# Adding up the seven products of a Winograd-form FFN-down matmul: three running sums kept as they are, one kept combined, and every addition on VectorE

## The chip, the cores and the metric

The kernel runs on one NeuronCore of a Trainium2 chip. The metric is the device time of one execution in microseconds (us); a lower time is better. A core has five engines that run side by side and wait for each other through semaphores: TensorE (PE; its weight loads are shown apart as PEld), VectorE (DVE), ScalarE (ACT), GpSimd (POOL) and SyncE (SP), which issues the DMAs here. Matmul results land in PSUM, from where VectorE and ScalarE read them; everything else lies in SBUF or in HBM.

## The reference

One layer of a diffusion backbone over 640 tokens (512 latent, 128 context): a mixer (gated DeltaNet and latent attention), then a gated convolutional FFN, then a final norm. The part that matters here is the end:

```python
def conv_ffn(h, w_up, conv_w, conv_b, w_down):
    u = depthwise_conv_centred(h @ w_up, conv_w) + conv_b
    a, gate = jnp.split(u, 2, axis=-1)
    return (jax.nn.silu(a) * gate) @ w_down
...
    x = x + gate2 * conv_ffn(h2, p['w_up'], p['ffn_conv_w'], p['ffn_conv_b'], p['w_down'])
```

D_MODEL is 2048 and D_FF is 5632, all in float32. `@ w_down` is the "down" stage: for each of 16 output tiles (128 features x 640 tokens) it sums over 44 tiles of 128 hidden features.

## The kernel before

**The seven products.** Down works on 2x2 blocks. A pair of output tiles p (8 pairs) and the two halves of the tokens (320 each) make four output quarters C11, C12, C21, C22 of 128x320; four hidden tiles at a time (index n, 11 of them) make the inner dimension. Instead of eight block products it computes seven, Q1 to Q7, from sums of weight blocks and sums of activation blocks (Winograd's form), and then combines them: C11 = Q1+Q2, C12 = Q1-Q6-Q5+Q3, C21 = -Q4-(Q1-Q6+Q7), C22 = Q5-(Q1-Q6+Q7), each summed over n. Float32 precision is kept by splitting every operand into a high and a low part (`split`, L921: a cast on ScalarE writes `whi` or `b_hi`, a subtraction on VectorE writes `wlo` or `b_lo`), and each product is three matmuls: hi by hi, hi by lo, and lo by hi.

**Units.** For one (p, n) the work is two units: R computes Q2, Q1, Q4, Q7 with the raw weight blocks (24 matmuls of 128x320 into two PSUM tiles named `mm`), S computes Q6, Q5, Q3 with the weight sums (18 matmuls into two PSUM tiles named `dn`). The table `blocks` (L1479) sets the order: a plain first block (4 units W, without Winograd), then blocks 1 to 8 with two n for each of four p, block 9 with three n and block 10 with two. Within a block PSUM accumulates over its n; so for every p, 40 times in all, the seven products have to be added to the running sums in SBUF before the next p may write the same PSUM. This text calls the work on one p of one block a round.

**The running sums** are tiles `x_hi`, `x_lo` and `xw` (the first two are named for the freed activation buffers that they occupy); c11, c12, c21, c22 are halves of two of them.

**Around it**, for each unit: `d_load` (L1528) brings 512 KB of weights into `wraw` (2 buffers); `d_sums` (L1533) makes three weight sums and one difference with four 128x256 additions on VectorE (tiles `us` and `vs`); `d_prep` (L1542) splits the weights (2 buffers of `whi`, `wlo`); `g_prep` (L1511), spread over a block by `g_steps`, makes four differences of activations per tile on GpSimd (L1518; tiles `ca`, `cg`, `rawa`, `rawg`, `graw`) and splits them; `residual2` (L1655) adds the gated result to x behind the last block of a p, with one GpSimd addition (L1670).

**The adding up** is `d_post` (L1607), called for the unit before the one whose matmuls were just issued. All its additions are recorded by the helper `add`, so they stand at line L1603, as do those of `d_sums`. Behind R, ScalarE copies Q1 and Q7 to tiles `x` and `y` (L1624, L1625) and VectorE adds Q2 and Q1 to c11 and subtracts Q4 from c21, three reads of PSUM. Behind S, VectorE makes x = x - Q6 and y = y + x, subtracts Q5 from c12, adds Q3 to c12 and Q5 to c22; GpSimd adds x to c12 and subtracts y from c21 and from c22. In block 1, where c11 to c22 of four p start, the first write replaces the sum (`new`).

**What sets the order.** A scheduler puts each engine's instructions into a fixed list when the program is built; each engine then goes through its list in order and waits where a semaphore is not yet there. PSUM tiles `mm` are single (two tags, one buffer each), so the first R of a round waits until VectorE and ScalarE have read the last R of the round before.

## Time and profile before

| | |
|---|---|
| median of 3 runs | 3340.32 us (3339.84 to 3347.75) |
| profiled execution, its own time | 3335.4 us |
| its span, first to last instruction | 3333.6 us |
| busy over the span: PE, DVE, ACT, POOL | 93%, 82%, 44%, 19% |
| mean granted TensorE clock | 0.965 of full speed |
| down stage in the trace | about 2684 to 3307 us |

A busy share says how long an engine's instructions ran, with the waiting inside an instruction counted as running. The down stage is the last fifth; the rows below are nearly all from it. "Idle before" is the time in which an engine stood still ahead of an instruction, put down to what released it.

### The profile page before, as it was taken

The numbers are of one execution on the slowest core, as the hardware profiler recorded it, in microseconds if no ns is written. First come the engines' busy times: TensorE is split into PE (matmuls) and PEld (weight loads), VectorE is DVE, ScalarE is ACT, GpSimd is POOL, SyncE is SP. The second block draws the span as 40 slices with busy tenths as digits, with TensorE's granted clock in tenths as the row PEclk, the third lists the DMA queues.
The fourth block names the chain that finished last, engine by engine and source line by source line (L and its number), as shares of the span: only waits on it lengthen the run. The fifth ranks groups of instructions, "written<-read, shape, count | busy, mean of one in ns | idle before, by whom it ended". The sixth has DMA issues, their size and how long they took to land. (4 is left out here: it accounts for less than half of the span.)

```text
span 3333.6 us, 54622 instructions
## 1 busy us (share of the span) xinstructions
PE 3099.1 (93%) x21243; PEld 2989.7 (90%) x21243; DVE 2721.6 (82%) x4626; ACT 1450.2 (44%) x2230; POOL 640.5 (19%) x456
## 2 busy tenths in 40 slices
PE   5889999999998998997999999999999989889996
PEld 4688989898998988997999999999999988888986
DVE  7766666866576667998998898898898889999988
ACT  5444555554446542115544444444444443333433
POOL 1211111211110001334100010000000044334323
PEclk9999999998899999998999999999999999999998
DMA  7652222323233217873333333333333333232333
GB/s 274 212 173 75 81 83 69 104 66 98 70 120 98 63 64 238 283 257 108 129 123 105 114 125 105 121 125 99 126 118 98 108 116 100 86 103 91 95 107 119
DMA packets 181475, 403.93 MB, mean 121 GB/s; under 512 B 39392, under 2 KB 57952, under 8 KB 181216
## 3 DMA queue, kind: packets, MB, share of 16 engines
q1 hardware_dynamic: 181216, 400.44, 37.3%
q8 instruction: 167, 2.74, 0.3%
q14 instruction: 92, 0.75, 0.1%
HBM read 361.83 MB, written 38.54 MB: 120 GB/s over the span
## 5 line engine op out<-in xcount | busy, mean ns | idle before, releaser
L922 ACT CAST whi<-wraw 128x1024 fp32r<-128x1024 f32 x256 | 268.9, 1050 | 521.6 <-PE mm L1596 200.4
L326 DVE SCALAR_TENSOR_TENSOR aacc<-araw,csil,aacc 128x512 f32<-128x512 f32 x510 | 397.3, 819 | 14.2 <-DMA araw<-in_w_ada_dram 13.7
L198 PE MATMUL mm<-b_hi,whi 128*128 128x320 f32 x1344 | 398.6, 310 | 4.7 <-ACT whi L922 3.9
L198 PE MATMUL mm<-b_lo,whi 128*128 128x320 f32 x1344 | 397.7, 310 | 0.0
L923 DVE TENSOR_TENSOR wlo<-wraw,whi 128x1024 fp32r<-128x1024 f32 x256 | 326.0, 1273 | 81.4 <-PE dn L207 63.0
L131 POOL TENSOR_TENSOR wlo<-wraw,whi 128x1024 fp32r<-128x1024 f32 x61 | 191.3, 3135 | 982.4 <-PE mm L207 553.0
L198 PE MATMUL mm<-h_hi,whi 128*128 128x320 f32 (+1 forms) x1312 | 326.7, 328 | 7.7 <-ACT h_hi L289 6.2
L198 PE MATMUL mm<-h_lo,whi 128*128 128x320 f32 (+1 forms) x1312 | 316.3, 321 | 12.5 <-POOL h_lo L290 12.5
L198 PE MATMUL dn<-b_lo,whi 128*128 128x320 f32 x1008 | 297.7, 309 | 0.0
L198 PE MATMUL dn<-b_hi,whi 128*128 128x320 f32 x1008 | 297.6, 309 | 0.0
L1596 PE MATMUL mm<-b_hi,whi 128*128 128x320 f32 x672 | 216.9, 335 | 60.2 <-DVE x_hi L1603 27.8
L129 ACT CAST whi<-wraw 128x1024 fp32r<-128x1024 f32 (+1 forms) x138 | 142.8, 1034 | 268.8 <-PE mm L198 164.8
L198 PEld LDWEIGHTS mm<-b_hi,whi 128*128 128x128 f32 x1344 | 253.2, 188 | 5.5 <-ACT whi L922 4.4
L198 PEld LDWEIGHTS mm<-b_lo,whi 128*128 128x128 f32 x1344 | 253.2, 188 | 0.0
L198 PEld LDWEIGHTS mm<-h_lo,whi 128*128 128x128 f32 x1312 | 227.5, 194 | 16.3 <-POOL h_lo L290 14.8
L198 PEld LDWEIGHTS mm<-h_hi,whi 128*128 128x128 f32 x1312 | 226.9, 195 | 13.3 <-ACT h_hi L289 8.2
L207 PE MATMUL mm<-h_hi,wlo 128*128 128x320 f32 (+1 forms) x1312 | 236.8, 322 | 0.0
L1456 POOL TENSOR_TENSOR y<-x,y 128x320 f32<-128x320 f32 x42 | 40.7, 968 | 977.1 <-DVE x L1454 977.1
L207 PE MATMUL mm<-b_hi,wlo 128*128 128x320 f32 x1344 | 224.4, 309 | 0.0
L922 ACT CAST whi<-us 128x1024 fp32r<-128x1024 f32 (+1 forms) x126 | 123.5, 980 | 230.8 <-PE mm L198 162.7
L1596 PE MATMUL mm<-b_lo,whi 128*128 128x320 f32 x672 | 210.0, 329 | 0.0
L207 PEld LDWEIGHTS mm<-h_hi,wlo 128*128 128x128 f32 x1312 | 206.4, 195 | 1.8
(534 smaller groups left out, 7895.0 us busy)
## 6 DMA issues: line engine op xcount, KB each, us to landing
wraw<-in_w_up_dram SPq DMA_DIRECT2D x176, 512.0 KB
araw<-in_w_ada_dram SPq DMA_DIRECT2D x272, 256.0 KB
wraw<-in_w_down_dram SPq DMA_DIRECT2D x88, 512.0 KB
wraw<-in_w_in_dram SPq DMA_DIRECT2D x80, 512.0 KB
araw<-in_w_ada_dram SPq DMA_DIRECT2D x56, 512.0 KB
wraw<-in_w_out_dram SPq DMA_DIRECT2D x32, 512.0 KB
graw<-g_d SPq DMA_DIRECT2D x44, 320.0 KB
g_d<-cg SPq DMA_DIRECT2D x44, 256.0 KB
```

Source lines behind the costliest of these rows:

```text
L129: act.copy(hi[:, :, 0:n], raw[:, :, 0:n])
L131: (pool if on_pool else dve).tensor_tensor(lo[:, :, 0:n], raw[:, :, 0:n], hi.bitcast(F32)[:, :, 0:n], ALU.subtract)
L198: pe.matmul(o, wts[0][:, k, col:col + P], m[:, sl], start=start and k + n == 0, stop=False)
L207: pe.matmul(o, wts[1][:, k, col:col + P], mov(k)[0][:, sl], start=False, stop=stop and k == 3)
L326: dve.scalar_tensor_tensor(acc[:, c, 0:w], raw, vecs[:, kt, c:c + 1], acc[:, c, 0:w], ALU.mult, ALU.add)
L922: act.copy(dst_hi, src)
L923: dve.tensor_tensor(dst_lo, src, dst_hi.bitcast(F32), ALU.subtract)
L1456: pool.tensor_tensor(y, x, y, ALU.add)
L1596: pe.matmul(dq[q], wt(w[0], k), bs[(2 * n + k) % 6][m][:, q, :], start=n == grp[0] and k + m == 0, stop=False)
```

## The change

Three things change in the down stage, and one tile is laid out differently in the up stage.

1. The running sums are C11, C12+C22, C21 and C22. Since C12+C22 = Q3 - Q7, no product is read twice: Q1 comes to c11 from ScalarE's copy, and Q5 goes to c22 alone. After the plain block c22 is added to c12 (4 additions), and after a p's last block it is subtracted again (8 additions).
2. `d_post` now only reads PSUM; a new `d_post2` does the additions between SBUF tiles, all on VectorE. x, y and z are three slices of one tile `xyz`, and ScalarE copies Q7 with its sign changed. So c11 and c12, where they lie side by side in one tile, take x and -Q7 in one addition of 128x640; c21 and c22 take the third slice in one 128x640 subtraction. For pair p = 6 they don't lie side by side, and there it is four of 128x320. In block 1 ScalarE copies Q2, Q4, Q3 and Q5 into the sums.
3. `d_sums` is called between `d_post` and `d_post2` and no longer in `d_prep`.

```diff
--- before.py
+++ after.py
@@ -1441,16 +1441,14 @@
         q24, q17, q53, q6 = (pq.get((p, n)) for n in (0, 1, 2, 6))
         half = (slice(0, CH), slice(512, 512 + CH))
         if g == 4:
-            x = cp.tile([P, CH], F32, name="x")
-            y = cp.tile([P, CH], F32, name="y")
-            tt[p] = (x, y)
+            xyz = cp.tile([P, 3, CH], F32, name="xyz")
+            tt[p] = x, y, _ = [xyz[:, n] for n in range(3)]
             act.copy(x, q17[:, half[0]])
             act.copy(y, q17[:, half[1]])
             dve.tensor_tensor(raws[0][:, 1:CH + 1], x, q24[:, half[0]], ALU.add)
             dve.tensor_tensor(raws[1][:, 1:CH + 1], y, q24[:, half[1]], ALU.subtract)
         if g == 6:
-            x, y = tt.pop(p)
-            z = cp.tile([P, CH], F32, name="z")
+            x, y, z = tt.pop(p)
             dve.tensor_tensor(x, x, q6[:, half[0]], ALU.add)
             dve.tensor_tensor(z, x, q53[:, half[0]], ALU.add)
             pool.tensor_tensor(y, x, y, ALU.add)
@@ -1552,7 +1550,6 @@
             split(hi, lo, draw[i])
             d_load(i + 2)
         if c != "R":
-            d_sums(i + 1)
             draw.pop(i)
         return hi, lo
 
@@ -1604,51 +1601,70 @@
 
     dt = {}
 
-    def d_post(u, q):
-
+
+
+    def d_done(u):
         i, c = units[u]
         b, p, n = order[i]
         if n != blocks[b][1][-1]:
+            return None
+        return c, b, p, n, [xh[2 * p + m // 2][m % 2] for m in range(4)]
+
+    def d_post(u, q):
+
+        if not d_done(u):
             return
+        c, b, p, n, (c11, c12, c21, c22) = d_done(u)
         if c == "W":
             for t, ps in zip((2 * p, 2 * p + 1), q):
                 for x, sl in x_pieces(t):
                     act.copy(x, ps[:, C0 + sl.start:C0 + sl.stop])
-            return
-        new = b == 1
-        c11, c12, c21, c22 = (xh[2 * p + m // 2][m % 2] for m in range(4))
-        if c == "R":
-            x = cp.tile([P, CH], F32, name="x")
-            y = cp.tile([P, CH], F32, name="y")
-            dt[p] = (x, y)
-            act.copy(x, q[Q1])
-            act.copy(y, q[Q7])
-            if new:
-                add(dve, c11, x, q[Q2])
-                dve.scalar_tensor_tensor(c21, y, -1.0, q[Q4], ALU.mult, ALU.subtract)
+        elif c == "R":
+            dt[p] = xyz = cp.tile([P, 3, CH], F32, name="xyz")
+            act.copy(xyz[:, 0], q[Q1])
+            act.activation(xyz[:, 1], q[Q7], AF.Copy, scale=-1.0)
+            if b == 1:
+                act.copy(c11, q[Q2])
+                act.activation(c21, q[Q4], AF.Copy, scale=-1.0)
             else:
                 add(dve, c11, c11, q[Q2])
-                add(dve, c11, c11, q[Q1])
                 add(dve, c21, c21, q[Q4], ALU.subtract)
+        else:
+            xyz = dt[p]
+            add(dve, xyz[:, 2], xyz[:, 0], q[Q6], ALU.subtract)
+            if b == 1:
+                act.copy(c12, q[Q3])
+                act.copy(c22, q[Q5])
+            else:
+                add(dve, c12, c12, q[Q3])
+                add(dve, c22, c22, q[Q5])
+
+    def d_post2(u):
+
+        if not d_done(u):
             return
-        x, y = dt.pop(p)
-        add(dve, x, x, q[Q6], ALU.subtract)
-        if new:
-            add(dve, c12, x, q[Q5], ALU.subtract)
-            add(pool, y, x, y)
-            add(dve, c12, c12, q[Q3])
-            add(pool, c21, c21, x, ALU.subtract)
-            add(dve, c22, q[Q5], y, ALU.subtract)
-        else:
-            add(dve, y, y, x)
-            add(dve, c12, c12, q[Q5], ALU.subtract)
-            add(dve, c12, c12, q[Q3])
-            add(dve, c22, c22, q[Q5])
-            add(pool, c12, c12, x)
-            add(pool, c21, c21, y, ALU.subtract)
-            add(pool, c22, c22, y, ALU.subtract)
-        if n == 10:
-            finish.append(p)
+        c, b, p, n, (c11, c12, c21, c22) = d_done(u)
+        if c == "W":
+            add(dve, c12, c12, c22)
+        elif c == "S":
+            xyz = dt.pop(p)
+            add(dve, xyz[:, 2], xyz[:, 2], xyz[:, 1], ALU.subtract)
+            y = xyz[:, 2]
+            if 2 * p in xw:
+                w = xw[2 * p].rearrange("p (h c) -> p h c", h=2)
+                add(dve, w, w, xyz[:, 0:2])
+            else:
+                add(dve, c11, c11, xyz[:, 0])
+                add(dve, c12, c12, xyz[:, 1])
+            if 2 * p + 1 in xw:
+                w = xw[2 * p + 1].rearrange("p (h c) -> p h c", h=2)
+                add(dve, w, w, y.unsqueeze(1).broadcast_to([P, 2, CH]), ALU.subtract)
+            else:
+                add(dve, c21, c21, y, ALU.subtract)
+                add(dve, c22, c22, y, ALU.subtract)
+            if n == 10:
+                add(dve, c12, c12, c22, ALU.subtract)
+                finish.append(p)
 
     finish, sq, xres = [], {}, {}
 
@@ -1792,6 +1808,10 @@
         w = w2
         if u:
             d_post(u - 1, q0)
+        if u + 1 < len(units) and units[u + 1][1] != "R":
+            d_sums(units[u + 1][0] + 1)
+        if u:
+            d_post2(u - 1)
         q0 = q
         if finish and units[u][1] == "S":
             done = finish.pop(0)
@@ -1805,6 +1825,7 @@
             r_load(0)
             r_load(1)
     d_post(len(units) - 1, q0)
+    d_post2(len(units) - 1)
     for i in range(2):
         sq[14 + i] = raws[i][:, 0:T]
     sums = ps_pair(0)
```

**In the instruction lists.** Counted over the down stage, VectorE had 312 additions of 128x320 for the adding up, 276 of them with a PSUM operand; it now has 256 of 128x320, 184 of them with a PSUM operand, and 70 of 128x640. GpSimd had 116 and has none. The up stage's lists are the same but for the tile's name.

VectorE, block 2, from the end of one round to the start of the next; `mm` and `dn` are PSUM. Before:

```order
L1603 TENSOR_TENSOR vs<-wraw,vs 128x256
L1603 TENSOR_TENSOR x_lo_26652<-x_lo_26652,mm_27709 128x320
L923 TENSOR_TENSOR wlo<-wraw,whi 128x1024
L1603 TENSOR_TENSOR x_lo_26652<-x_lo_26652,mm_27710 128x320
L1603 TENSOR_TENSOR x_lo_26652<-x_lo_26652,mm_27709 128x320
L1603 TENSOR_TENSOR x<-x,dn 128x320
L923 TENSOR_TENSOR wlo<-us,whi 128x768
L1603 TENSOR_TENSOR y<-y,x 128x320
L1603 TENSOR_TENSOR x_lo_26652<-x_lo_26652,dn 128x320 x3
L1603 TENSOR_TENSOR us<-wraw 128x256
L1603 TENSOR_TENSOR us<-us,wraw 128x256
```

Now:

```order
L1600 TENSOR_TENSOR x_lo_26570<-x_lo_26570,mm_27618 128x320
L923 TENSOR_TENSOR wlo<-wraw,whi 128x1024
L1600 TENSOR_TENSOR x_lo_26570<-x_lo_26570,mm_27618 128x320
L1600 TENSOR_TENSOR vs<-wraw,vs 128x256
L1600 TENSOR_TENSOR xyz<-xyz,dn 128x320
L923 TENSOR_TENSOR wlo<-us,whi 128x768
L1600 TENSOR_TENSOR x_lo_26570<-x_lo_26570,dn 128x320 x2
L1600 TENSOR_TENSOR xyz<-xyz 128x320
L1600 TENSOR_TENSOR x_lo_26570<-x_lo_26570,xyz 128x640 x2
L923 TENSOR_TENSOR wlo<-wraw,whi 128x1024
L1600 TENSOR_TENSOR us<-wraw 128x256
L1600 TENSOR_TENSOR us<-us,wraw 128x256
```

Between the split of the next R (`wlo<-wraw`) and the last read of `mm` stood two reads, and now one; behind the split of the next S (`wlo<-us`) stood y and three reads of `dn`, and now two reads, one addition of 128x320 and two of 128x640.

GpSimd, in blocks 6 and 7: `ca` and `cg` belong to the two activation tiles of one step. Before:

```order
L1518 TENSOR_TENSOR ca<-graw,ca 128x320
L1518 TENSOR_TENSOR rawa<-ca,graw 128x320
L1603 TENSOR_TENSOR xw_26654<-xw_26654,y 128x320
L1603 TENSOR_TENSOR xw_26653<-xw_26653,x 128x320
L1603 TENSOR_TENSOR xw_26654<-xw_26654,y 128x320
L1603 TENSOR_TENSOR x_hi_26649<-x_hi_26649,y 128x320
L1603 TENSOR_TENSOR x_hi_26649<-x_hi_26649,x 128x320
L1603 TENSOR_TENSOR x_hi_26649<-x_hi_26649,y 128x320
L1518 TENSOR_TENSOR cg<-graw 128x320
L1518 TENSOR_TENSOR graw<-graw 128x320
L1518 TENSOR_TENSOR cg<-graw,cg 128x320
```

Now:

```order
L1516 TENSOR_TENSOR ca<-graw,ca 128x320
L1516 TENSOR_TENSOR rawa<-ca,graw 128x320
L1516 TENSOR_TENSOR cg<-graw 128x320
L1516 TENSOR_TENSOR graw<-graw 128x320
L1516 TENSOR_TENSOR cg<-graw,cg 128x320
```

The six additions between the two groups of four are gone, and the groups follow each other.

ScalarE, block 1, the end of the first round. Before:

```order
L922 CAST whi<-wraw 128x1024
L1624 COPY x<-mm_27015 128x320
L1625 COPY y<-mm_27015 128x320
L922 CAST whi<-us 128x768
L922 CAST whi<-wraw 128x1024
L922 CAST whi<-vs 128x768
```

Now:

```order
L922 CAST whi<-wraw 128x1024
L1627 COPY x_hi_26567<-mm_26928 128x320
L1624 COPY xyz<-mm_26929 128x320
L1625 ACTIVATE xyz<-mm_26929 128x320
L1628 ACTIVATE x_hi_26567<-mm_26928 128x320
L922 CAST whi<-us 128x768
L1636 COPY x_hi_26567<-dn 128x320
L1637 COPY x_hi_26567<-dn 128x320
L922 CAST whi<-wraw 128x1024
```

ScalarE now reads all of the first block's PSUM tiles but Q6.

## Rows read from the trace of the kernel before

**Rows 1.** windows: whole down stage, a free round, one block (columns as headed).
```profile
core 0: us, PE busy (x) PEld busy (x) DVE busy (x) ACT busy (x) POOL busy (x), PEclk, DMA share, GB/s
2684.00:3307.00 623.00, 558.69 (x3557) 544.72 (x3556) 565.23 (x915) 236.59 (x342) 235.06 (x198) 0.96 0.30 96
2850.70:2863.00 12.30, 12.30 (x86) 12.30 (x85) 11.93 (x21) 8.83 (x15) 3.73 (x3) 1.00 0.35 112
2850.70:2909.10 58.40, 52.47 (x338) 50.88 (x337) 55.40 (x89) 22.12 (x33) 21.74 (x20) 0.97 0.29 95
```

**Rows 2.** waits, 2690 to 3310: engine line waited for: total us, times, longest.
```profile
PE mm L1596 <- DVE x_hi L1603: 27.8, 18, 3.0
...
PE mm L1596 <- DVE x_lo L1603: 15.6, 7, 3.0
...
PE mm L1596 <- ACT xw L1616: 8.0, 1, 8.0
...
PE mm L1596 <- DVE x_hi L1628: 3.5, 2, 2.6
```

**Rows 3.** lines by form, DVE, down stage: xcount | busy us, mean ns | idle before.
```profile
L923 DVE TENSOR_TENSOR wlo<-wraw,whi 128x1024 fp32r<-128x1024 f32 x84 | 115.8, 1379 | 18.4 <-PE mm L1599 13.4 <-ACT whi L922 2.1 <-ACT cg L1668 1.8
L923 DVE TENSOR_TENSOR wlo<-vs,whi 128x768 fp32r<-128x768 f32 x42 | 44.5, 1059 | 7.2 <-PE dn L1599 7.2
...
L923 DVE TENSOR_TENSOR b_lo<-graw,b_hi 128x640 fp32r<-128x640 f32 x38 | 36.9, 974 | 0.0
L1603 DVE TENSOR_TENSOR us<-wraw 128x256 f32<-128x256 f32 x41 | 31.3, 764 | 4.6 <-DMA wraw<-in_w_down_dram 4.6
...
L1603 DVE TENSOR_TENSOR x_hi<-x_hi,mm 128x320 f32<-128x320 f32 x57 | 26.1, 476 | 0.0
...
L1603 DVE TENSOR_TENSOR vs<-wraw,vs 128x256 f32<-128x256 f32 x42 | 18.1, 431 | 0.0
L1603 DVE TENSOR_TENSOR y<-y,x 128x320 f32<-128x320 f32 x35 | 16.8, 480 | 0.0
...
L923 DVE TENSOR_TENSOR b_lo<-ca,b_hi 128x640 fp32r<-128x640 f32 x9 | 7.3, 810 | 0.0
```

**Rows 4.** line L1603 alone, down stage: duration ns shortest/median/longest.
```profile
L1603 DVE TENSOR_TENSOR x_hi<-x_hi,mm x57: 472/475/489, 2765.9 to 3292.4; 128x320 f32<-128x320 f32 x57
...
L1603 DVE TENSOR_TENSOR us<-wraw x41: 408/743/1102, 2700.0 to 3279.7; 128x256 f32<-128x256 f32 x41
...
L1603 POOL TENSOR_TENSOR x_lo<-x_lo,y x41: 866/887/1866, 2771.1 to 3297.3; 128x320 f32<-128x320 f32 x41
```

**Rows 5.** the weight splits alone, down stage, the same columns.
```profile
L923 DVE TENSOR_TENSOR wlo<-wraw,whi x84: 1207/1224/1939, 2690.5 to 3298.5; 128x1024 fp32r<-128x1024 f32 x84
```

**Rows 6.** timeline, 2898.9 to 2902.7: start us, us, engine line op names.
```profile
2898.91 1.40 DVE L1603 TENSOR_TENSOR x_lo<-x_lo,dn 128x320 f32<-128x320 f32 x3
...
2899.06 0.87 POOL L1603 TENSOR_TENSOR x_lo<-x_lo,y 128x320 f32<-128x320 f32 x1 [5.48 <-DVE y L1603]
...
2899.99 0.87 POOL L1603 TENSOR_TENSOR x_lo<-x_lo,x 128x320 f32<-128x320 f32 x1
2900.22 0.91 DVE L1603 TENSOR_TENSOR us<-wraw 128x256 f32<-128x256 f32 x1
```

**Rows 7.** windows of line L1603 alone, down stage.
```profile
core 0: us, DVE busy (x) POOL busy (x), PEclk, DMA share, GB/s
2684.00:3307.00 623.00, 312.00 (x636) 125.07 (x113) 0.96 0.30 96
```

**Rows 8.** windows of line L1518 alone (GpSimd differences of activations), down stage.
```profile
2684.00:3307.00 623.00, 0.00 (x0) 81.43 (x72) 0.96 0.30 96
```

**Rows 9.** lines by form, ACT, down stage.
```profile
L1625 ACT COPY y<-mm 128x320 f32<-128x320 f32 x40 | 17.3, 431 | 0.0
```

**Rows 10.** the chain that ended last, its piece behind the last product.
```profile
3306.60 0.50 DVE x L1603
...
3307.69 0.87 POOL xw L1603
```

## The prediction

> **What bounds the kernel now.** The up stage's instruction lists stay as they are, so I read the down stage only, first by windows. Over its 623 us TensorE is busy for 558.7, VectorE for 565.2 and GpSimd for 235.1 [rows 1]: two engines are nearly full, and neither sets the pace alone. A free round shows TensorE's pace: 12.30 us, busy throughout at the full clock [rows 1], for 84 matmuls, so 0.146 us each. One steady block of four rounds takes 58.4 us, 9.2 more than four times 12.30 = 49.2. [...] VectorE is idle for only 3.0 of the 58.4.
>
> The waits, read next, tell what TensorE stands idle for: VectorE's additions to the running sums, 27.8 + 15.6 us in 25 times, then 8.0 behind ScalarE's copies of the plain block and 3.5 in block 1 behind L1628 [rows 2]. All are the first matmul on `mm`: a round cannot start before the last round's R products are read. In VectorE's list that last read stands behind a weight split and two other reads.
>
> Third, why VectorE is late. Groups by form, against the shortest of their kind, show that some of its instructions run far longer than they need: the first weight sum takes 764 ns in the mean [rows 3] and 408 at best [rows 4], while a read of PSUM takes 476 [rows 3], with 472 and 489 as ends [rows 4]. The timeline shows what lies beside the long ones: three reads of PSUM run through while GpSimd works, 1.40 us for three, but a sum of two SBUF tiles of 256 columns takes 0.91 us behind GpSimd's addition [rows 6].
>
> **The change, part by part.** All durations are of the profiled execution, 3335.4 us with a span of 3333.6; the median shown is 3340.3, so what comes out below is subtracted from the median too.
>
> *VectorE's own work: +30 us.* Before, 312 additions by 0.476 [rows 3] are 148.5 us. Now 256 by 0.476 are 121.9, and 70 of 640 columns by 0.810 (the subtraction `b_lo<-ca` has that width [rows 3]) are 56.7; together 178.6. An addition without PSUM costs the same as one with it (`y<-y,x` 480 [rows 3]), so trading one for the other is free by itself.
>
> [...]
>
> *GpSimd's additions beside VectorE: -43 us.* Mean less shortest, by count: the seven groups of weight sums (first and last in rows 3, shortest about 408 [rows 4]) come to 61 us, the R weight splits to 84 x (1379 - 1207) = 14 [rows 3, 5], the activation splits to 38 x (974 - 810) = 6 [rows 3]; 81 us in all that VectorE's instructions are held up beside GpSimd. GpSimd is busy 125.1 us with the adding up [rows 7] out of 235.1 [rows 1]: 53%, so 43 us. Ends: 19, if each of the 72 activation differences [rows 8] already holds VectorE for its whole 0.866 [rows 4], 62 us; and 81, if they hold nothing.
>
> *More VectorE work that GpSimd can hold up: +7 us.* What is left of GpSimd's work (81.4 us of differences [rows 8] and 13 residual additions) now costs 81 - 43 = 38. Before, 276 x 0.476 = 131 of VectorE's 565 us were reads of PSUM, which are not held up; now it is 184 x 0.476 = 88. So 77% of its time was exposed and 84% will be: +4. The wide additions are the longest exposed ones, so I take +7. Ends: -3, when the groups of four, no longer queued behind additions that wait for y, fall into VectorE's idle tenth; and +34, when each of the 72 holds it for a whole 0.866 (62 instead of their share of 38, which is 28).
>
> VectorE's load thus changes by 30 - 43 + 7 = -6 us, with ends at -51 (30 - 81) and +21 (30 - 43 + 34). One round in four is bound by TensorE, as the free one is; three quarters count: **-4.5**.
>
> *One read fewer before the release: -8.* Between the split of the next R and the last read of `mm` stood two reads, now one; a read in a row takes about 0.45 (1.40 for three [rows 6]). TensorE waited there 25 times [rows 2]: 11 us at most. In a round that VectorE fills from end to end the place in the list does not matter, so I take two thirds. Behind the next S split the list gets longer (four instructions of 0.45 before, three and two of about 0.75 now: +1.0), in a place where `mm` is already free; it is covered as long as TensorE's R and S units, 42 x 0.146 = 6.1 us, run beside it.
>
> *Block 1: -3.* Its reads of `mm` go to ScalarE, four of 0.431 [rows 9] are 1.7 us, covered by the S unit's 18 x 0.146 = 2.6. The 3.5 us behind L1628 [rows 2] should nearly go.
>
> *Plain block: +1.* Four more VectorE additions are 1.9 us if its list there is full; TensorE's 8.0 wait hangs on ScalarE and stays. Between 0 and 1.9. *Tail: +1.* From VectorE's x at 3306.60 to the end of GpSimd's addition at 3308.56 [rows 10] it is 2.0 us; now four additions of 0.45 and two of 0.75 stand there, 3.3. Nothing covers it.
>
> *Clock: -4.* The whole stage needs 3720 matmuls (84 times 42, and 192 of the plain block) x 0.146 = 545 us and TensorE is busy 558.7: 14 us at the lower level beside 55 of waits, 0.25 per us of wait. On -4.5 - 8 - 3 that is -4.
>
> Sum: -4.5 - 8 - 3 + 1 + 1 - 4 = -17.5, say -17. Profiled 3318, median **3323 us**. ScalarE's extra copies (16 of 128x320, and a sign at no cost) are hidden: it is busy 237 of 623 [rows 1].
>
> **The rivals.**
>
> *Larger gain, 3303.* If the additions taken from GpSimd had cost VectorE 60 rather than 43 and nothing comes back, the load falls by 30, x 0.75 = -22; the full 11 for the read, -3, +2 and a quarter of 36 for the clock make -43. VectorE would then more often be ahead of its weights (it waits 4.6 us for their DMA before one of the sums even now [rows 3]), so I call it -37. For it: the long sums lie right behind GpSimd's additions [rows 6]. Against: three fifths of the stage's GpSimd instructions cannot well cost three quarters of the delay.
>
> *No change, 3338.* The wait moves: the weight sums now stand behind the reads and, for `us`, behind the wide additions too, and ScalarE's cast of the next R waits for their last difference. TensorE then waits for `whi` instead of `mm`, the 8 and the clock's share are lost, and -2 remains. For it: VectorE is as full as before. Against: a cast of weights is not among TensorE's largest waits today [rows 2].
>
> *Slower, 3365.* The remaining differences, in uninterrupted groups of four, hold up the wide additions. If all 72 cost their 0.866, VectorE's load rises by 21 and it is behind in every round, so all of it counts, with a quarter for the clock: +26, no gain from the order, -3 + 2: +25. It decides from 13 us of growth instead of my 7, where the load stops falling. For it: VectorE has 3.0 of 58.4 us to spare. Against: today's differences cost 28 of 62.
>
> [...]
>
> **How the numbers follow.** Within 0.3%, 10 us, this kernel's measurement cannot be told from no change. Forecast 0.46 (own range 3313 to 3333: faster 0.38, same 0.08); no change 0.27 (same 0.22, faster 0.03, slower 0.02); larger 0.15 (faster); slower 0.12 (slower 0.10, same 0.02). Together 0.56, 0.32 and 0.12. The range 3299 to 3348 takes in the forecast, no change and most of the larger gain, and leaves out the slower rival's far end.
>
> **What would show it.** Right: the weight sums' means near 550 ns or less, VectorE busy about 560 us in the stage, TensorE's waits for L1603's successors under 30 us, no wait at block 1, wide additions at 0.81 to 0.95 in the mean. Wrong: wide additions above 1.1 us in the mean (slower), or TensorE waiting for `whi` (no change). The up stage must end at 2684 as before; if it does not, the difference isn't in this argument.

## The result, and the profile after

The changed kernel takes 3301.5 us (median of 4 runs, 3283.3 to 3303.2), the kernel before 3342.1 in the same series: ratio 0.9864, 95% interval 0.9827 to 0.9901, so it is 33 to 58 us faster; the medians differ by 41. The forecast was 17 faster: the direction was right, its size less than half of the measured one.

First the place. This row shows the first matmuls of the plain block (ns shortest, median and longest, then the starts of the first and the last in us), of the kernel before:

```profile
L1572 PE MATMUL mm<-b_hi,whi x32: 304/309/413, 2659.4 to 2683.0; 128*128 128x320 f32 x32
```

and of the changed kernel:

```profile
L1569 PE MATMUL mm<-b_hi,whi x32: 309/309/414, 2674.2 to 2697.7; 128*128 128x320 f32 x32
```

The down stage starts 14.8 us later after the change, though nothing ahead of it was to change. The change is not needed to explain that: in the fourteen other traces below, whose instructions are nearly the same up to there, the stage starts anywhere from 2662 to 2677, and 14 of the 14.8 us arise in the first 300 us of the program. The plain block itself takes 28.5 us in both. So I compare the forty rounds, from the last matmul of the plain block to the last product, by windows; the kernel before:

```profile
core 0: us, PE busy (x) PEld busy (x) DVE busy (x) ACT busy (x) POOL busy (x), PEclk, DMA share, GB/s
2688.00:3307.10 619.10, 554.79 (x3530) 541.05 (x3530) 561.32 (x912) 236.13 (x341) 231.22 (x195) 0.96 0.30 96
```

and the changed kernel, one steady block and all rounds:

```profile
2861.60:2912.20 50.60, 49.91 (x339) 49.44 (x339) 50.06 (x90) 22.21 (x33) 10.81 (x8) 1.00 0.36 110
2702.70:3269.70 567.00, 532.02 (x3528) 525.76 (x3528) 536.70 (x921) 240.01 (x354) 112.75 (x82) 0.98 0.34 105
```

The rounds take 567.0 instead of 619.1: -52.1. What follows them, the tail, takes 30.7 instead of 26.5. Together that is -48 in one trace of each kernel, against -41 of the medians with an interval 25 wide, so the rounds hold the whole effect as far as these can tell. A block that took 58.4 [rows 1] takes 50.6, with TensorE (49.9) and VectorE (50.1) both nearly full.

TensorE's waits in the rounds of the changed kernel (total us, times, longest), which answer to [rows 2]:

```profile
PE mm L1593 <- DVE x_lo L1600: 9.5, 9, 5.2
PE mm L1593 <- ACT xw L1621: 8.8, 1, 8.8
PE mm L1593 <- DVE x_hi L1600: 7.0, 5, 2.5
PE mm L1593 <- ACT whi L922: 4.0, 3, 1.4
PE mm L1593 <- DVE xyz L1600: 3.6, 2, 1.9
```

Behind x_hi and x_lo it is 16.5 instead of 43.4, block 1 has none, and the plain block's wait behind ScalarE stays (8.8). VectorE's groups by form (count | busy, mean ns | idle before), which answer to [rows 3]:

```profile
L923 DVE TENSOR_TENSOR wlo<-wraw,whi 128x1024 fp32r<-128x1024 f32 x84 | 107.8, 1283 | 9.8 <-ACT whi L922 6.0 <-PE mm L1596 3.5
...
L1600 DVE TENSOR_TENSOR x_hi<-x_hi,xyz 128x640 f32<-128x640 f32 x30 | 25.0, 861 | 0.0
...
L1600 DVE TENSOR_TENSOR x_lo<-x_lo,xyz 128x640 f32<-128x640 f32 x30 | 23.6, 814 | 0.0
L1600 DVE TENSOR_TENSOR vs<-wraw 128x256 f32<-128x256 f32 x42 | 22.3, 532 | 13.4 <-DMA wraw<-in_w_down_dram 13.4
...
L1600 DVE TENSOR_TENSOR xyz<-xyz,dn 128x320 f32<-128x320 f32 x40 | 19.1, 479 | 0.5 <-PE dn L1596 0.2
...
L1600 DVE TENSOR_TENSOR us<-wraw 128x256 f32<-128x256 f32 x41 | 17.1, 416 | 2.1 <-DMA wraw<-in_w_down_dram 2.0
```

The first weight sum of `us` is down from 764 ns to 416, the R weight split from 1379 to 1283; a read of PSUM is what it was, 479; the wide additions are scarcely held up, 861 and 814 ns against the 810 that were forecast. Most of the signs that the prediction named have come; the size has not.

I keep the books by VectorE: the length of the rounds is its busy time plus its idle time. (That holds for any engine; that VectorE is the right one is shown by the runs with spare work below.) Busy fell by 24.6 (561.3 to 536.7), idle by 27.5 (57.8 to 30.3).

The busy part I take apart as the forecast did. "Own work" is each instruction at the shortest duration of its kind: 530.6 to 558.2, +27.6. "Held up" is what instructions ran beyond that, scatter of under some 50 ns left out: 88.3 to 40.6, -47.7. Put down to the GpSimd instruction that ran beside (good to 1 or 2 us), 39.8 of it were GpSimd's additions, which are gone; its differences went from 37.7 to 32.4, its residual sums from 10.8 to 8.1. The remaining -4.5 is mostly that neighbours in VectorE's list overlap more: their durations add up to 60.8 us more than the busy time before and 67.4 now, with some 2 of scatter against it.

The idle part was in the trace of before, in its waits of VectorE in the rounds:

```profile
DVE vs L1603 <- DMA wraw<-in_w_down_dram: 21.2, 16, 2.8
DVE wlo L923 <- PE mm L1599: 13.4, 20, 1.8
DVE wlo L923 <- PE dn L1599: 8.4, 14, 1.4
DVE us L1603 <- DMA wraw<-in_w_down_dram: 4.6, 5, 2.2
```

and is this in the changed kernel:

```profile
DVE vs L1600 <- DMA wraw<-in_w_down_dram: 13.4, 7, 3.1
DVE wlo L923 <- ACT whi L922: 6.9, 8, 2.7
DVE wlo L923 <- PE mm L1596: 3.5, 3, 2.4
DVE us L1600 <- DMA wraw<-in_w_down_dram: 2.0, 2, 1.3
```

With the short ones that these views leave out, waits for weights fell from 25.8 to 15.5 and waits for TensorE from 25.2 to 6.2. One place in the changed kernel shows what a wait for weights does; the timeline of SyncE, VectorE and TensorE (start, length, [idle before]):

```profile
2772.29 1.21 DVE L923 TENSOR_TENSOR wlo<-wraw,whi 128x1024 fp32r<-128x1024 f32 x1
...
2773.53 9.10 SPq L1529 DMA_DIRECT2D wraw<-in_w_down_dram  x2
...
2778.11 0.62 DVE L1600 TENSOR_TENSOR vs<-wraw 128x256 f32<-128x256 f32 x1 [1.61 <-DMA wraw<-in_w_down_dram]
2778.77 0.97 DVE L1600 TENSOR_TENSOR vs<-vs,wraw 128x256 f32<-128x256 f32 x1
2779.66 1.08 DVE L1600 TENSOR_TENSOR wraw<-wraw 128x256 f32<-128x256 f32 x1
2780.66 0.47 DVE L1600 TENSOR_TENSOR x_hi<-x_hi,mm 128x320 f32<-128x320 f32 x1
2781.05 1.21 DVE L923 TENSOR_TENSOR wlo<-wraw,whi 128x1024 fp32r<-128x1024 f32 x1
2782.19 0.48 DVE L1600 TENSOR_TENSOR x_lo<-x_lo,mm 128x320 f32<-128x320 f32 x1
...
2782.81 0.61 PE L1593 MATMUL mm<-b_hi,whi 128*128 128x320 f32 x1 [5.18 <-DVE x_lo L1600]
```

The split ends at 2773.50 and frees the raw weights' buffer, the load is issued 0.03 later, and the sum that needs it stands only some 3.0 us of work further on in VectorE's list, while this load takes 4.6. The sum waits 1.61. Three sums, each longer than its shortest 0.41, and a split stand ahead of the last read of `mm`; TensorE waits 5.18.

### The profile page after: what moved, and what is told of

It is laid out like the page before. It is cut to its first block, busy times and chain, and to the rows that moved or that the text cites. A ratio compares the mean times of both kernels' runs of the same rounds, so it can differ in the third digit from the quotient of the medians.

```text
span 3300.4 us, 54485 instructions
## 1 busy us (share of the span) xinstructions
PE 3083.5 (93%) x21243; PEld 2981.0 (90%) x21243; DVE 2697.6 (82%) x4640; ACT 1454.6 (44%) x2246; POOL 528.6 (16%) x340
## 5 line engine op out<-in xcount | busy, mean ns | idle before, releaser
L326 DVE SCALAR_TENSOR_TENSOR aacc<-araw,csil,aacc 128x512 f32<-128x512 f32 x510 | 398.4, 822 | 17.4 <-DMA araw<-in_w_ada_dram 17.1
L198 PE MATMUL mm<-b_hi,whi 128*128 128x320 f32 x1344 | 398.8, 310 | 4.0 <-ACT whi L922 3.3
L923 DVE TENSOR_TENSOR wlo<-wraw,whi 128x1024 fp32r<-128x1024 f32 x256 | 318.0, 1242 | 72.0 <-PE dn L207 62.1
L198 PE MATMUL mm<-h_lo,whi 128*128 128x320 f32 (+1 forms) x1312 | 320.6, 324 | 21.0 <-POOL h_lo L290 20.9
L1593 PE MATMUL mm<-b_hi,whi 128*128 128x320 f32 x672 | 205.3, 319 | 33.5 <-DVE x_lo L1600 9.5
L207 PEld LDWEIGHTS mm<-b_hi,wlo 128*128 128x128 f32 x1344 | 204.7, 188 | 0.0
```

Of the source, the lines that this page charges most:

```text
L198: pe.matmul(o, wts[0][:, k, col:col + P], m[:, sl], start=start and k + n == 0, stop=False)
L207: pe.matmul(o, wts[1][:, k, col:col + P], mov(k)[0][:, sl], start=False, stop=stop and k == 3)
L326: dve.scalar_tensor_tensor(acc[:, c, 0:w], raw, vecs[:, kt, c:c + 1], acc[:, c, 0:w], ALU.mult, ALU.add)
L923: dve.tensor_tensor(dst_lo, src, dst_hi.bitcast(F32), ALU.subtract)
L1593: pe.matmul(dq[q], wt(w[0], k), bs[(2 * n + k) % 6][m][:, q, :], start=n == grp[0] and k + m == 0, stop=False)
```

## The experiments

The columns, in us: the forty rounds; VectorE busy, of that held up, and idle; of the idle what waits for weights; "short", the number of first weight sums (of 82) with under 3.3 us of work in VectorE's list between the split that frees their buffer and themselves; the median, and the ratio, with its interval, to the kernel before as it ran in the same series (3342.1 to 3345.9). The 3.3 is near the least that a load took: sums that waited started 3.18 to 5.25 us behind their load's issue, half of them over 3.57. A sum near the bound can fall on either side: counted with the shortest durations of these traces, before has 29 and a_narrow 11.

| kernel | rounds | busy | held up | idle | weights | short | median | ratio |
|---|---|---|---|---|---|---|---|---|
| before | 619.1 | 561.3 | 88.3 | 57.8 | 25.8 | 31 | 3342.1 | 1 |
| before_again | 619.6 | 562.8 | 90.0 | 56.8 | 26.7 | 31 | 3340.7 | one run |
| b_sums_behind | 602.7 | 566.2 | 95.8 | 36.5 | 16.9 | 15 | 3326.9 | 0.9955 (0.9941 to 0.9969) |
| b_read_less | 602.6 | 561.0 | 91.9 | 41.6 | 27.1 | 33 | 3328.5 | 0.9960 (0.9946 to 0.9975) |
| b_no_gpsimd | 575.0 | 554.1 | 40.9 | 20.9 | 5.1 | 3 | 3308.7 | 0.9892 (0.9873 to 0.9911) |
| **after** | 567.0 | 536.7 | 40.6 | 30.3 | 15.5 | 16 | 3301.5 | 0.9864 (0.9827 to 0.9901) |
| a_gpsimd_adds | 662.5 | 569.0 | 127.4 | 93.5 | 80.2 | 65 | 3398.5 | 1.0164 (1.0147 to 1.0180) |
| a_sums_first | 569.0 | 538.5 | 42.9 | 30.5 | 15.6 | 16 | 3298.9 | 0.9865 (0.9844 to 0.9886) |
| a_sums_later | 562.2 | 542.3 | 46.6 | 19.9 | 15.5 | 8 | 3298.2 | 0.9857 (0.9836 to 0.9878) |
| a_narrow | 561.6 | 538.4 | 39.2 | 23.2 | 12.1 | 15 | 3293.1 | 0.9845 (0.9825 to 0.9865) |
| a_diff_vector | 542.7 | 528.9 | 8.2 | 13.8 | 3.0 | 5 | 3271.8 | 0.9785 (0.9763 to 0.9807) |
| a_gpsimd_beside | 611.5 | 583.7 | 89.1 | 27.8 | 10.4 | 16 | 3343.4 | 0.9998 (0.9983 to 1.0012) |
| a_beside_p01 | 591.0 | 559.5 | 63.2 | 31.5 | 12.3 | 16 | 3324.5 | 0.9937 (0.9914 to 0.9960) |
| a_beside_p23 | 591.7 | 561.4 | 65.2 | 30.3 | 11.4 | 16 | 3322.1 | 0.9929 (0.9906 to 0.9951) |
| a_vector_beside | 612.8 | 581.4 | 39.5 | 31.4 | 6.1 | 6 | 3344.4 | 1.0006 (0.9992 to 1.0019) |

**before_again**: no edit, a second trace.

> The kernel before, unchanged, for a second trace of it. In the first one the first 300 us passed 12 us faster than in the traces of five other kernels whose instructions are the same up to there, and the down stage began at 2659 instead of 2672 to 2677. If that was this one execution, the second trace has the stage begin at 2668 to 2678 and the forty rounds take 612 to 625 us again, and the change is worth more in the stage (52 us) than in the profiled total (33). If it is a property of the kernel, the stage begins near 2659 again.

The stage starts at 2664.2, between the two places that were expected; the rounds take 619.6. So in this one pair of traces the rounds repeat to 0.5 us, and what comes ahead of them differs by 4.7.

The diffs below are excerpts: `...` stands for lines left out, and the comments in them are not in the kernels.

**Single parts of the change on the kernel before.** b_sums_behind moves the call of the weight sums:

```diff
-            d_sums(i + 1)                    # in d_prep
...
+        if u + 1 < len(units) and units[u + 1][1] != "R":
+            d_sums(units[u + 1][0] + 1)      # behind d_post(u - 1, q0)
```

> The kernel before with one move: the four weight sums stand behind the reads of PSUM of the S unit instead of ahead of them; GpSimd keeps its additions. Theory 'order' (the changed kernel's gain came from VectorE reading PSUM before the work that can wait, and my forecast, which priced the sums' move at nothing, missed it): 12 to 25 us faster than before, TensorE's waits for L1603's additions in the down stage fall from 50 us to under 30, and VectorE's busy time there stays near 566 us. Theory 'contention' (GpSimd's additions held VectorE up for more than the 43 us of the forecast): within 5 us of before, since GpSimd works as it did.

It is faster by 15 us (10 to 20), the rounds by 16.4. Busy rose by 4.9 and idle fell by 21: there are 15 short distances instead of 31, 9 us less wait for weights, and 10 less for TensorE. My forecast had priced this move at nothing.

**b_read_less** takes one read of PSUM off the release:

```diff
-                add(dve, c11, c11, q[Q1])    # R unit
...
+        if not new:
+            add(dve, c11, c11, x)            # S unit, ahead of x -= Q6
```

> The kernel before with one read of PSUM moved off the way: C11's addition of Q1 is taken from ScalarE's copy x, in the S unit ahead of x's own update, so that only two reads of PSUM stand between the next R split and the release of mm, as in the changed kernel. Same number and length of VectorE's additions. My forecast's term: 8 us faster, 11 at most. Theory 'order' in the form that this read alone is the mis-sized term: 15 to 25 us faster, TensorE's waits for L1603 under 30 us. Theory 'contention': 3 us or less.

It is faster by 13 us (8 to 18). The rounds of its trace are 16.5 shorter, above the 11 that I had put as the most, but the interval of the times takes in 11 and even 8. VectorE's waits for TensorE went from 25.2 to 7.7; its busy time stayed, and so nearly did its waits for weights.

**b_no_gpsimd** is the engine alone:

```diff
-            add(pool, c12, c12, x)           # five such lines in d_post
+            add(dve, c12, c12, x)
...
```

> The kernel before with the adding up that GpSimd did (113 additions of 320 columns) given to VectorE in the same places; nothing else moved. My forecast's terms: VectorE's own work +113 x 0.476 = 54 us, GpSimd's hold-up -43, so load +11, and about 8 to 11 us slower than before. Theory 'contention' (all 81 us of hold-up hung on these additions): load -27, 20 to 27 us faster. Theory 'order': as the forecast, slower by 5 to 15.

It is faster by 36 us (30 to 42), where my terms gave 8 to 11 slower; the other two theories missed as well. The rounds' row:

```profile
2700.30:3275.30 575.00, 533.96 (x3528) 522.35 (x3528) 554.12 (x1022) 234.98 (x339) 125.96 (x81) 0.99 0.33 103
```

VectorE has 110 more instructions, and yet its busy time is 7 lower, since it is held up 47 less. Its idle time is 37 lower, 21 of that in waits for weights: in its list only 3 first sums stand too close behind their split. So this one part alone takes 44 of the 52 us off the rounds, and five sixths of that is idle time.

**a_gpsimd_adds** is the opposite, on the changed kernel: the additions to the running sums go back to GpSimd, 640 wide where they are so in the changed kernel.

```diff
-                add(dve, w, w, xyz[:, 0:2])  # all additions of d_post2 behind z - y
+                add(pool, w, w, xyz[:, 0:2])
...
```

> The changed kernel with its wide additions to the running sums put on GpSimd, in the same places of the program; the order of the reads, the sums and the additions stays, and so does VectorE's z-y. VectorE's own work falls by about 70 x 0.81 = 57 us, the hold-up beside GpSimd grows by some 40 to 60. Theory 'order': as fast as the changed kernel or up to 12 us faster (3290 to 3303). Theory 'contention': the gain of the change is lost, 20 to 40 us slower than the changed kernel, near 3330.

It is slower than the changed kernel by 97 us, far beyond both theories. VectorE's waits in the rounds:

```profile
DVE vs L1600 <- DMA wraw<-in_w_down_dram: 64.4, 40, 3.6
DVE us L1600 <- DMA wraw<-in_w_down_dram: 15.7, 17, 3.6
```

The scheduler now puts 65 of 82 sums too close behind their split. Busy time is 32 higher in spite of some 67 us less of own work, idle time 63 higher; that makes the 95.5 by which the rounds are longer.

**The order of the calls, on the changed kernel.** a_sums_first and a_sums_later move the call of the weight sums:

```diff
+        if u + 1 < len(units) and units[u + 1][1] != "R":      # a_sums_first
+            d_sums(units[u + 1][0] + 1)
         if u:
             d_post(u - 1, q0)
-        if u + 1 < len(units) and units[u + 1][1] != "R":
-            d_sums(units[u + 1][0] + 1)
+        if units[u][1] != "R" and u + 1 < len(units):          # instead, a_sums_later
+            d_sums(units[u + 1][0])
```

> The changed kernel with the weight sums called ahead of the reads of PSUM, as before the change; all else as changed. In VectorE's list 202 of 1452 rows stand elsewhere, but as many first weight sums as in the changed kernel (16 of 82) have less than 3.3 us of work between the split that frees the buffer and themselves. Theory 'order of the calls' (reads ahead of the sums are worth 12 us or more also here): 10 to 20 us slower than the changed kernel. Theory 'list' (what counts is this distance): within 5 us of the changed kernel.

There is no difference (rounds +2, median -3). The place of this call was worth 15 us in the kernel before and is worth nothing here; the lists go with it, 31 short distances against 15 there, 16 against 16 here.

> The changed kernel with the four weight sums called one unit later, with the R unit of the same n as the next work, so that they have a whole unit more for their weights and less time ahead of their own split: in VectorE's list 8 of 82 first sums instead of 16 have less than 3.3 us of work behind the split that frees their buffer. Theory 'list': VectorE's waits for weights fall from 15 us to 9 or 10, the kernel 4 to 8 us faster than the changed one, unless TensorE then waits for whi of the S unit. Theory 'order of the calls': no faster, and 5 to 15 us slower if the sums now stand between the R split and the reads that release mm.

(Here the R split takes the fourth raw block without its sum.) The median is 3 lower and the rounds 5, which the intervals do not tell apart from the changed kernel. The waits for weights did not fall to 9 or 10, since the move changed what frees the buffer. One place, VectorE and SyncE:

```profile
2733.64 1.22 DVE L923 TENSOR_TENSOR wlo<-wraw,whi 128x1024 fp32r<-128x1024 f32 x1
...
2735.11 0.42 DVE L1600 TENSOR_TENSOR wraw<-wraw 128x256 f32<-128x256 f32 x1
2735.60 0.33 SPq L1529 DMA_DIRECT2D wraw<-in_w_down_dram  x1
...
2739.08 0.42 DVE L1600 TENSOR_TENSOR vs<-wraw 128x256 f32<-128x256 f32 x1 [2.68 <-DMA wraw<-in_w_down_dram]
```

Sums of the same weights now stand behind the split, and the load is issued 0.07 behind the last of them. In 82 of 84 cases it comes more than 0.2 us behind the split, 1.2 in the mean; in the changed kernel it comes 0.03 behind in all. Counted from the instruction that frees the buffer, 11 sums and not 8 are short, and what they lack to 3.3 us adds up to 15.3, against 15.5 that VectorE waited.

**Hold-up alone.** a_gpsimd_spare adds GpSimd work on a spare tile with no tie to a round:

```diff
+            for _ in range(3):
+                add(pool, dt["spare"], dt["spare"], dt["spare"])
```

> The changed kernel with three additions of 320 columns on GpSimd in each round on a spare tile that nothing else reads; VectorE's list is the same, instruction for instruction. So GpSimd is as busy as before the change, but nobody waits for it and no place in VectorE's list moves. Theory 'hold-up' (GpSimd's additions cost what they hold VectorE up by, 40 us in the trace of before, and VectorE's load counts in full): 35 to 50 us slower than the changed kernel, 3337 to 3352. Theory 'list' (a good part of the cost of GpSimd's additions was that the scheduler, which counts their time, then put the first weight sum right behind the split that frees its buffer, so that VectorE waited for the reload, which takes 3.3 us): 15 to 30 us slower, and VectorE's waits for weights stay near the 15 us of the changed kernel.

It took 3363.0 and does not answer the question: the additions run in one heap, from 2652 to about 2800, beside the plain block and the first rounds. The window of the plain block:

```profile
2665.00:2727.00 62.00, 35.01 (x192) 33.98 (x192) 37.03 (x40) 13.01 (x19) 57.94 (x64) 0.72 0.23 71
```

The plain block takes 61 us instead of 28.5 there, the first rounds some 30 more, and the later rounds pass as in the changed kernel. So a_gpsimd_beside ties them to the round by what they read:

```diff
+            for m in (c12, c21, c22):        # behind VectorE's wide additions
+                add(pool, dt["spare"], m, m)
```

> The changed kernel with three additions of 320 columns on GpSimd in each round that read the running sums just after VectorE's wide additions and write a spare tile which nobody reads: as many as GpSimd had before the change, now beside the same stretch of the round, with VectorE's list the same, instruction for instruction. Theory 'hold-up' (the additions cost what they hold VectorE up by, about 40 us, and all of it counts): 35 to 50 us slower than the changed kernel, 3337 to 3352. Theory 'list' (a good part of their cost was where the scheduler then put the weight sums): 10 to 25 us slower, 3312 to 3327.

It is slower than the changed kernel by 42 and level with before: 120 additions (117 of them within the rounds) cost the whole gain. VectorE's list is the same instruction for instruction, and it waits for these additions 3.7 us in all, where it writes a sum that they still read. The rounds' row, VectorE's first weight sum by form, and one of its reads of PSUM (ns shortest, median, longest):

```profile
2701.40:3312.90 611.50, 549.12 (x3529) 537.84 (x3528) 583.69 (x921) 240.08 (x356) 315.49 (x200) 0.96 0.31 98
...
L1600 DVE TENSOR_TENSOR us<-wraw 128x256 f32<-128x256 f32 x41 | 27.7, 677 | 0.3 <-DMA wraw<-in_w_down_dram 0.2
...
L1600 DVE TENSOR_TENSOR xyz<-xyz,dn x40: 470/474/489, 2727.3 to 3312.4; 128x320 f32<-128x320 f32 x40
```

The first sum went from 416 ns to 677, the read of PSUM stayed; busy rose by 47.0, the rounds by 44.5. So a microsecond of hold-up costs about a microsecond here, not three quarters.

**a_vector_beside** puts the same additions on VectorE (`add(dve, ...)`).

> The changed kernel with the three spare additions of each round (120 of 320 columns, on a tile that nobody reads) on VectorE, where a_gpsimd_beside had them on GpSimd and lost 42 us. VectorE's own work grows by 120 x 0.476 = 57 us of durations, some 48 us of its list. Theory 'load' (a microsecond of VectorE's time costs the same whether it works or is held up, as my forecast's sum had it): 36 to 50 us slower than the changed kernel, 3337 to 3352, as on GpSimd. Theory 'heaps' (own work is spread over all rounds and falls into their slack, hold-ups come in heaps that a round cannot take): 0 to 18 us slower, 3300 to 3320.

It is slower than the changed kernel by 43. Its row:

```profile
2698.10:3310.90 612.80, 547.14 (x3528) 535.70 (x3528) 581.38 (x1038) 239.06 (x355) 129.72 (x82) 0.96 0.31 97
```

Busy rose by 44.7, the rounds by 45.8. The theory of heaps falls: own work counts in full as well. (VectorE's list also differs in other places: it waits 9 us less for weights and 8 more for ScalarE.) **a_beside_p01** and **a_beside_p23** keep the spare GpSimd additions in half of the rounds (`for m in (c12, c21, c22) if p % 4 < 2 else ()`, and `> 1`).

> Of the 120 spare GpSimd additions of a_gpsimd_beside only those in the rounds of the first two p of each block, 60, where GpSimd's differences stand as well; VectorE's list is that of the changed kernel. Theory 'heaps': these are the dear ones, 25 to 38 of the 42 us, 3327 to 3340. If hold-ups cost the same in every round: half, 21 us, 3322.

> The other 60 of the spare GpSimd additions, in the rounds of the last two p of each block, where GpSimd has no differences; VectorE's list is that of the changed kernel. Theory 'heaps': a round takes them, 2 to 14 us slower than the changed kernel, 3304 to 3316. If hold-ups cost the same in every round: half, 21 us, 3322.

They are 23 and 21 us slower than the changed kernel, with 22.8 and 24.7 more of busy time: half each, wherever the additions stand. So in four runs on the changed kernel, what VectorE's busy time gains the rounds gain, nearly one to one.

**a_narrow** splits the wide additions again:

```diff
-                add(dve, w, w, xyz[:, 0:2])
...
+            add(dve, c11, c11, xyz[:, 0])
+            add(dve, c12, c12, xyz[:, 1])
...
```

> The changed kernel with each addition of 640 columns as two of 320: VectorE's own work grows by 70 x (2 x 0.476 - 0.81) = 10 us, GpSimd's stays. The first weight sums stand about as in the changed kernel (15 of 82 instead of 16 under 3.3 us). My forecast's price of VectorE's load (three quarters, and a quarter for the clock): 8 to 10 us slower than the changed kernel, 3309 to 3312. If VectorE's load is not what sets the time any more: within 4 us of it.

Its median is 8 us lower, not higher, though the intervals overlap. Busy rose by only 1.7: in the changed kernel's trace an addition of 320 columns lasts 0.48 us, but the next instruction starts 0.40 behind it, and one of 640 takes 0.73 to the next start, so 70 more instructions overlap 70 more times. Idle fell by 7. No gain from the widening is shown.

**a_diff_vector** takes GpSimd's differences off too:

```diff
-            (eng or pool).tensor_tensor(o, x, y, ALU.subtract)
+            (eng or dve).tensor_tensor(o, x, y, ALU.subtract)
```

> The changed kernel with GpSimd's differences of the activations (L1516) on VectorE too. VectorE's own work grows by 70 to 80 x 0.476 = 33 to 38 us, and the 32 us by which these differences hold it up go. In VectorE's list 5 of 82 first weight sums instead of 16 have less than 3.3 us of work behind the split that frees their buffer. Theory 'hold-up': the two cancel, within 5 us of the changed kernel. Theory 'list': VectorE's waits for weights fall from 15 us to under 5, and the kernel is 8 to 20 us faster than the changed one, 3282 to 3294.

This is the fastest of all: 3271.8, 72 us (65 to 79) under before and some 26 to 30 under the changed kernel. Its rounds:

```profile
2692.50:3235.20 542.70, 526.86 (x3529) 518.72 (x3527) 528.86 (x985) 237.18 (x348) 26.39 (x12) 1.00 0.35 109
```

VectorE is held up 8 us instead of 41 and has some 30 more of own work; its busy time is 8 lower. It waits 3 us for weights instead of 15, and its idle time is 16 lower. TensorE's granted clock is 1.00. Both theories named a part that is there: a third of the gain is busy time, two thirds are idle time, and of these most is waits for weights.

## Why the prediction was wrong, step by step

In the forecast's sum, load, order, clock and block 1 came to -19.5 and the plain block and the tail to +2. In the traces, VectorE's busy time gives -24.6, its idle time -27.5 and the tail +4.2.

*Own work, +30.* Right: +27.6. *GpSimd's additions, -43.* Right: 39.8 of hold-up beside them is gone.

*More work that GpSimd can hold up, +7.* Wrong in sign: the hold-up beside the differences and residual sums fell by 8. In the fourteen traces with the differences on GpSimd (a_gpsimd_spare left out) their hold-up lies between some 20 and 38 us, and it is hardly larger where VectorE has more to hold up (a_vector_beside, 33.8, against 32.4). What GpSimd holds up, a_gpsimd_beside shows: beside its spare work the reads of PSUM stay at 470 to 489 ns, and the first weight sum, which reads SBUF alone, goes from 416 to 677 in the mean. That it would hit the wide additions often was my estimate: in the changed kernel they took 861 and 814 in the mean, though the last two were held up (the tail, below).

*Load -6, three quarters count: -4.5.* This is the step that failed. The load fell by 24.6: of the difference 15 lies in the term just named and 4 in the overlap of neighbours, net of scatter, for which the sum had no term. And a change of load counts in full, at least in the changed kernel: a_gpsimd_beside, a_vector_beside and the two halves have +47.0, +44.7, +22.8 and +24.7 of busy for +44.5, +45.8, +24.0 and +24.7 of rounds. I had taken one round in four as TensorE's from one block.

*One read fewer, -8, at most 11.* Here a term is missing rather than mis-sized. b_read_less alone gives 13 us (8 to 18), which does not refute the 8, though the 16.5 of its rounds speaks for more. What I left out is VectorE's own idle time, 57.8 us in the rounds: I had read it in one steady block, 3.0 of 58.4 [rows 1], and called VectorE full, while the idle column of its groups had 18.4 ahead of the R split [rows 3] and 21 ahead of `vs`. A late read makes TensorE late, and then VectorE waits for TensorE; b_read_less took 17.5 us off VectorE's waits for TensorE.

The weights' wait, 25.8, stood in no term at all, and neither did the place of the first sum in the list. The lists before and after, with a load's time from the trace of before, show it without any further run: 31 of 82 too close, then 16. Over the kernels of the table the time lacking to 3.3 us, summed from the lists, goes with the measured wait: 33.8 for 25.8, 17.1 for 16.9, 5.9 for 5.1, 12.4 for 15.5, 72.4 for 80.2, 2.0 for 3.0, and in a_sums_later 15.3 for 15.5.

How the 27.5 of idle splits is not settled. 10 is waits for weights and 19 waits for TensorE, while 3 more go to ScalarE; but either of b_read_less and b_no_gpsimd alone removes 17 to 20 of the waits for TensorE, so those shares overlap. That GpSimd's additions spoil the list because the scheduler counts their time is read from the lists, not tested by itself.

*Block 1, -3, and plain block, +1.* As said: the 3.5 went, and the 8.0 became 8.8. The sign on ScalarE's copy of Q7 was not quite free: 442 ns in the mean against 431 for the plain copy of before, 40 times, so 0.4 us. *Tail, +1.* It was 4.2: the two last wide additions take 2.72 us instead of 1.5 beside GpSimd's residual sum, and TensorE waits 2.7 for that sum.

*Clock, -4.* In the rounds the traces show half of the full clock granted for 54.6 us before and for 23.9 in the changed kernel; at half, matmuls that follow each other start 0.267 us apart, and at the full clock 0.147 (medians). That waits bring the clock down, on which the term's 0.25 per us of wait rests, is not shown by any run; it was my estimate. The matmuls' own busy time fell by 22.8 at the same count. I had set 3720 matmuls against a window that lists 3557 [rows 1]; the plain block lay mostly ahead of 2684. With 3557 the factor would have been (558.7 - 519) / 55 = 0.7 per us of wait, not 0.25, and the two traces show 22.8 less busy time beside 29.3 less idle time of TensorE. In VectorE's books this is no further term: it lies within the 52.1.

Of the rivals, the larger gain has the time, 3303, but not for its reasons, so that is luck: its "nothing comes back" was right, its 60 us for the additions (39.8), its three quarters and its longer waits for weights (they fell) were not. The slower one fails by the wide additions, no change by `whi`, for which TensorE waits 4.0.

## What to carry to other kernels

Keep the books by the engine that is busy or waited for in every round: take its busy time and its idle time over the whole stage, not from one block, and ask of each idle row what the change does to it. Where a scheduler writes the order, compare the two lists for the distance between an instruction that frees a buffer and the one that needs its reload; it can be counted before any run. Count from the last instruction that uses the buffer. And work on a helper engine that holds up the full one can cost as much as the same work on the full one, as the 120 spare additions did here (42 and 43 us).

## What the runs showed of the hardware

GpSimd's additions seem to be held up as well. In a_gpsimd_beside (ns shortest, median, longest) a spare addition takes 718 at best and 1235 in the median, as far as spans of that engine can be read; that it is VectorE that holds them is not shown by itself:

```profile
L1600 POOL TENSOR_TENSOR spare<-x_lo x60: 718/1235/6123, 2744.9 to 3307.1; 128x320 f32<-128x320 f32 x60
```

Spare work on GpSimd is as dear here as the same work on VectorE itself, 42 and 43 us for the 120 additions. A load of 512 KB of weights took 3.18 to 5.25 us from its issue to the start of the sum that waited for it. And the part of the program ahead of the down stage differs by up to 18 us between executions (2659 to 2677), while the forty rounds of the kernel before repeated to 0.5 us in two traces.
